# Output gates of a hybrid mLSTM/GLA encoder layer computed with features in partitions and applied after the transpose

## Chip, cores, metric

The kernel runs on one core of one Trainium2 chip. The metric is device time in microseconds (us), the median of several runs. One further execution was taken by the hardware profiler; all rows below come from it.

## What is computed

One layer of a bidirectional encoder over 1024 tokens of width 1024, in float32. The part that matters here is the output of the token mixer:

```python
y_a = sigmoid(a_o) * head_rms_norm(h_fw + h_bw, mlstm_norm)   # 4 heads x 128
y_b = silu(b_r)    * head_rms_norm(o_fw + o_bw, gla_norm)     # 4 heads x 128
y   = concatenate([y_a, y_b], axis=-1)
mix = matmul(y, w_out)
x   = x + rms_norm(mix, norm_mix_post)
```

`a_o` and `b_r` are two 512-column parts of one input projection of the normalised `x`. `head_rms_norm` multiplies each head's 128 features of a token by one number, and by a gain per feature (the kernel folds that gain into `w_out`). A gated MLP with a width-3 convolution follows; the change does not touch it.

## The kernel before

Matmuls in float32 are made of three with a rounded operand each: an operand `v` is split into `vh` (a rounded copy, made by ScalarE, L112) and `vl = v - vh` (VectorE, L113), and the product is `vh*wh + vh*wl + vl*wh`.

**Stages.** First `x` is normalised and transposed to `xh`, `xl` (features in partitions). From then on two generators are interleaved by `_interleave`: `proj()` emits the blocks of the input projection, `mix()` emits the decays, the GLA heads (`gla`), then the mLSTM heads (`mlstm`), and at last the preparation of `w_out` (`out_weights`). Both write to the same five engines, so the projection's matmuls fill TensorE (PE) between the heads' small ones. The tile scheduler then sets the order in which each engine's in-order queue gets its instructions. After that comes the output projection, token tile by token tile (`t` = 0 to 7, 128 tokens each), and then the MLP.

**Blocks of the projection.** `f_block` gives 128 features (in partitions) by 512 tokens: the weights stand still in the array, `x` moves in 512 columns, 8 x 3 = 24 matmuls. `t_block` gives 2 x 128 tokens (in partitions) by 256 features: `x` stands still, the weights move in 256 columns, 2 x 8 x 3 = 48 matmuls. Both fill one PSUM bank. The gates `a_o` and `b_r` are the last 16 blocks of `proj()` and are `t_block`s: `in_gate` takes each bank through tanh on ScalarE (L480) and one more instruction (L482 on ScalarE for the sigmoid, L484 on VectorE for the silu), and after every second block stores 512 KB to `dG` in DRAM, tokens in rows.

**Applying the gates.** `prep(t)` loads the head outputs of one token tile, `yv` (from `dya`, L890, and `dyb`, L891), and its gates `gv` (L893), multiplies by gate and by the head's scale `hr` (eight instructions on VectorE, L897, one for each head), transposes the eight 128x128 blocks on PE in two groups of four (L903) and splits each group from PSUM into `yh`, `yl` for the output matmuls (`oacc`, L1019). In the loop over `t` (L1051 to L1071) the matmuls of tile `t` stand in two halves of 24; `prep(t+1)`'s two groups of transposes are put after the first half and in the middle of the second; after tile `t`, `post(t)` computes the norm (gain L984, power on GpSimd L1032, residual L1040, a second power) and `gates(t+2)` starts the loads of tile `t+2`. `scaled` writes `om` (L989, needs the second power); `finish` transposes it (L997).

**Buffers.** `yv` and `om` share one tag with two buffers. From tile 2 on they alternate, so all of `yv(2)`, `yv(3)`, ... lie in the same buffer, and the load of `yv(t+1)` has to wait for the last reader of `yv(t)`. `gv` has one buffer. All loads and stores around here are issued by SyncE's queue (SP), in order.

```python
yv = ow["p"].tile([P, D], F32, name="yv", tag="yv", bufs=2)
gv = ow["p"].tile([P, D], F32, name="gv", tag="gv", bufs=1)
m = owp.tile([P, D], F32, name="om", tag="yv", bufs=2)
```

Of the kernel before, what the change touches and what calls it, by code (L numbers as in the profile page):

```python
# [13 lines left out]
ALU = mybir.AluOpType  # L14
# [42 lines left out]
def tile_encoder_layer(  # L57
# [24 lines left out]
    dG = [scratch(f"dG{i}", [512, D]) for i in range(2)]  # L82
# [28 lines left out]
    def split(hi, lo, src):  # L111
        nc.scalar.copy(out=hi, in_=src)  # L112
        nc.vector.tensor_tensor(out=lo, in0=src, in1=hi.bitcast(F32), op=ALU.subtract)  # L113
# [294 lines left out]
    def ahead(b=1):  # L408
        c = next(groups, None) if b == 1 else None
        if c is not None:  # L410
            ready.append(wprep(w_in, ((c, 256),)))
# [58 lines left out]
    def in_gate(c0, off, silu):  # L470
        for g in range(2):
            wh, wl = ready.pop(0)
            yield
            for q in range(4):
                if q % 2 == 0:
                    s = stg.tile([P, 4, 256], F32, name="stg")
                acc = yield from t_block(wh, wl, q)
                ahead(q)
                v = s[:, 2 * (q % 2):2 * (q % 2) + 2, :]
                nc.scalar.activation(v, acc, AF.Tanh, scale=0.5)  # L480
                if not silu:
                    nc.scalar.activation(v, v, AF.Identity, bias=one)  # L482
                else:
                    nc.vector.scalar_tensor_tensor(out=v, in0=v, scalar=1.0, in1=acc, op0=ALU.add, op1=ALU.mult)  # L484
                if q % 2:
                    nc.sync.dma_start(dG[q // 2].rearrange("(t p) n -> p t n", p=P)[:, :, off + 256 * g:off + 256 * g + 256], s)
                    if silu and g == 1:
                        done["half"] = True
                yield
# [398 lines left out]
    def prep(t):  # L888
# [3 lines left out]
        gv = ow["p"].tile([P, D], F32, name="gv", tag="gv", bufs=1)  # L892
        nc.sync.dma_start(gv, dG[t // 4][(t % 4) * P:(t % 4 + 1) * P, :])  # L893
        for i in range(2):
            for h in range(H):
                hs = slice(512 * i + P * h, 512 * i + P * h + P)
                nc.vector.scalar_tensor_tensor(out=yv[:, hs], in0=gv[:, hs], scalar=hr[:, t, i, h:h + 1], in1=yv[:, hs], op0=ALU.mult, op1=ALU.mult)  # L897
        ys[t] = []
        for g in range(2):
# [8 lines left out]
            split(yh, yl, pt)  # L908
            ys[t].append((yh, yl))

    def proj():
# [9 lines left out]
        yield from in_gate(C_BR, 512, True)  # L921
# [410 lines left out]
```

## Time and profile before

| | us |
|---|---|
| median of 3 runs | 1188.94 (1188.13 to 1193.38) |
| the profiled execution | 1186.0 |
| its span, first to last instruction | 1184.2 |
| PE busy | 1149.1 (97%) |
| VectorE (DVE) busy | 880.3 (74%) |
| ScalarE (ACT) busy | 591.4 (50%) |
| GpSimd (POOL) busy | 165.5 (14%) |

The stages by time: normalisation and first projection 0 to 47 us, projection with decays and GLA to about 297, mLSTM to about 412, output weights to about 434, output projection to about 549, MLP to the end. The gates' 16 blocks lie between 270 and 433 us.

In a row of the timeline the columns are start, duration, engine, line, operation, written tile `<-` read tiles, and in brackets how long the engine had been idle and what ended that. PE durations overlap, since matmuls are pipelined: the pace is read from start to start, or from a row that merges a run of matmuls.

### The profile page before, as it was taken

The page shows a single profiled execution, that of the slowest core. Times are in us where ns is not written, and L with a number is a line of the kernel's source. Part 1 is how long each engine was busy: PE and PEld are TensorE (multiplying, and loading weights), DVE is VectorE, ACT ScalarE, POOL GpSimd, SP SyncE. Part 2 cuts the span into 40 slices and gives each one's busy share as a digit, 9 for nine tenths or more (in the row PEclk, how much of TensorE's full clock was granted, in tenths as well). Part 3 has the DMA queues.
Part 4 walks back from the last instruction along what each step waited for, and adds up shares of the span by engine and source line. Part 5 has one row for each costly group of instructions (what it writes and reads, how often), then busy time and mean ns, then how long its engine had stood idle before and what let it go on. Part 6 is the DMA issues. An engine that isn't in the chain of part 4 may idle for free.

```text
span 1184.2 us, 21224 instructions
## 1 busy us (share of the span) xinstructions
PE 1149.1 (97%) x7896; PEld 977.0 (82%) x7896; DVE 880.3 (74%) x1604; ACT 591.4 (50%) x1271; POOL 165.5 (14%) x240
## 2 busy tenths in 40 slices
PE   8999999999999989999999999999999999999997
PEld 7989778888989978777788888888888878888885
DVE  6576679777424567567998888888888877987666
ACT  6572696777556534456444243333434245445451
POOL 1200434665154200010000000000000000000001
PEclk9999999999989989999999999999999999999999
DMA  7453675554787485431144332242323248754345
GB/s 211 140 138 98 172 230 150 149 170 129 195 197 222 153 265 185 159 140 64 36 142 143 125 125 74 96 134 99 105 65 133 98 137 295 252 176 132 80 135 190
DMA packets 134651, 175.77 MB, mean 148 GB/s; under 512 B 24964, under 2 KB 89860, under 8 KB 134548
## 3 DMA queue, kind: packets, MB, share of 16 engines
q1 hardware_dynamic: 134116, 172.58, 47.7%
q0 software_dynamic: 432, 1.84, 0.4%
q8 instruction: 62, 1.02, 0.4%
q14 instruction: 41, 0.34, 0.1%
HBM read 126.78 MB, written 47.53 MB: 147 GB/s over the span
## 4 chain that ended last, share of the span: by engine, by line
PE 76%; DVE 6%; ACT 6%; DMA 5%; issue 3%; POOL 2%; SPq 1%; DVEq 0%; POOLq 0%; ACTq 0%
PE pr L1080 35%; PE pr L1238 17%; PE tacc L182 6%; PE facc L171 6%; PE oacc L1019 4%; PE vacc L262 2%; DMA yv<-dya 1%; DMA oraw<-in_w_out_dram 1%; DMA qq<-dmqq 1%; DVE slots L539 1%; PE sc L658 1%; ACT RB L792 1%; DMA wraw<-in_w_in_dram 1%; POOL RB L788 1%; ACT sq L545 1%
## 5 line engine op out<-in xcount | busy, mean ns | idle before, releaser
L1080 PE MATMUL pr<-T,ah 128*128 128x512 f32 x704 | 217.1, 389 | 1.3 <-DVE G L1118 1.3
L1080 PE MATMUL pr<-B,ah 128*128 128x512 f32 x528 | 162.8, 389 | 0.0
L1080 PEld LDWEIGHTS pr<-T,ah 128*128 128x128 f32 x704 | 132.1, 188 | 29.5 <-DVE G L1118 1.8
L1080 PE MATMUL pr<-T,al 128*128 128x512 f32 x352 | 136.9, 389 | 0.0
L182 PE MATMUL tacc<-wh,xh 128*128 128x256 f32 x448 | 130.6, 292 | 0.0
L182 PE MATMUL tacc<-wl,xh 128*128 128x256 f32 x448 | 130.0, 290 | 0.0
L182 PE MATMUL tacc<-wh,xl 128*128 128x256 f32 x448 | 127.0, 284 | 0.0
L1238 PE MATMUL pr<-dwl,dah 128*128 128x512 f32 x308 | 120.0, 390 | 0.7 <-DVE dwl L113 0.7
L1238 PE MATMUL pr<-dwh,dal 128*128 128x512 f32 x308 | 120.1, 390 | 0.0
L1238 PE MATMUL pr<-dwh,dah 128*128 128x512 f32 x308 | 119.2, 390 | 0.4 <-ACT dah L112 0.4
L1080 PEld LDWEIGHTS pr<-B,ah 128*128 128x128 f32 x528 | 99.0, 188 | 20.5
L1080 PE MATMUL pr<-B,al 128*128 128x512 f32 x264 | 102.7, 389 | 0.0
L112 ACT CAST dah<-ar 128x512 fp32r<-128x512 f32 x77 | 47.8, 622 | 97.2 <-PE pr L1238 44.5
L182 PEld LDWEIGHTS tacc<-wh,xh 128*128 128x128 f32 x448 | 85.5, 191 | 2.7 <-issue 0.2
L182 PEld LDWEIGHTS tacc<-wl,xh 128*128 128x128 f32 x448 | 85.6, 191 | 1.4
L182 PEld LDWEIGHTS tacc<-wh,xl 128*128 128x128 f32 x448 | 85.6, 191 | 0.3
L112 ACT CAST ah<-fraw 128x512 fp32r<-128x512 f32 x64 | 39.6, 619 | 82.0 <-PE pr L1080 53.7
L113 DVE TENSOR_TENSOR dal<-ar,dah 128x512 fp32r<-128x512 f32 x77 | 52.9, 689 | 35.5 <-ACT dah L112 35.4
L1080 PEld LDWEIGHTS pr<-T,al 128*128 128x128 f32 x352 | 66.1, 188 | 13.6
L112 ACT CAST ah<-sa 128x512 fp32r<-128x512 f32 x44 | 27.3, 621 | 84.0 <-DVE sa L960 53.3
L1238 PEld LDWEIGHTS pr<-dwl,dah 128*128 128x128 f32 x308 | 57.8, 188 | 13.1 <-DVE dwl L113 1.1
L1238 PEld LDWEIGHTS pr<-dwh,dah 128*128 128x128 f32 x308 | 57.8, 188 | 12.7 <-ACT dah L112 0.8
(292 smaller groups left out, 2528.8 us busy)
## 6 DMA issues: line engine op xcount, KB each, us to landing
ar<-dA SPq DMA_DIRECT2D x77, 256.0 KB
wraw<-in_w_in_dram SPq DMA_DIRECT2D x48, 256.0 KB
fraw<-in_ffn_w_gate_dram SPq DMA_DIRECT2D x22, 512.0 KB
fraw<-in_ffn_w_up_dram SPq DMA_DIRECT2D x22, 512.0 KB
dA<-s SPq DMA_DIRECT2D x20, 512.0 KB
dA<-sx SPq DMA_DIRECT2D x10, 768.0 KB
Y<-in_ffn_w_down_dram SPq DMA_DIRECT2D x22, 256.0 KB
S<-dS SPq DMA_DIRECT2D x16, 258.0 KB
```

Of the source, the lines that this page charges most:

```text
L112: nc.scalar.copy(out=hi, in_=src)
L113: nc.vector.tensor_tensor(out=lo, in0=src, in1=hi.bitcast(F32), op=ALU.subtract)
L171: nc.tensor.matmul(acc, w[:, k, cs], v[:, k, hs], start=(k == 0 and n == 0), stop=(k == NK - 1 and n == 2))
L182: nc.tensor.matmul(acc[:, i, :], v[:, k, ts], w[:, k, :], start=(k == 0 and n == 0), stop=(k == NK - 1 and n == 2))
L262: nc.tensor.matmul(acc, v[:, k, ts], w[:, k, :], start=(k == 0 and n == 0), stop=(k == NK - 1 and n == 2))
L539: nc.vector.scalar_tensor_tensor(out=sl[rs, o, h, :], in0=sl[rs, c, h, :], scalar=sc(c, h)[rs], in1=sl[rs, o, h, :], op0=ALU.mult, op1=ALU ...
L545: nc.scalar.activation(sq, o[:, h, :], AF.Square, accum_out=ss[:, h:h + 1])
L658: nc.tensor.matmul(sc[bs, h, :], K[:, h, bs], Q[:, h, bs], start=True, stop=True)
L788: nc.gpsimd.tensor_tensor(out=RB, in0=RB, in1=cap.rearrange("p (i o t) -> p i o t", i=2, o=1).broadcast_to([P, 2, H, P]), op=ALU.add)
L1019: nc.tensor.matmul(accs[hf], v[:, j, :], w[:, k, hf * 512:(hf + 1) * 512], start=(k == 0 and n == 0), stop=(k == NK - 1 and n == 2))
L1080: nc.tensor.matmul(acc, A[i][:, k, :], B[b][j][:, k, :], start=(k == 0 and n == 0), stop=(k == 3 and n == 2))
L1238: nc.tensor.matmul(accs[i], o[v][:, ts], o[w], start=(p == 0 and n == 0), stop=(p == NP - 1 and n == 2))
```

## The change

The 16 gate blocks become `f_block`s: 24 matmuls of 512 columns in place of 48 of 256, in the order `hf` (half of the tokens) outside, `j` (128 features) inside. ScalarE's and VectorE's work on each bank is the same in shape and number. `dG` now holds features in rows, 512 tokens in each. In `prep`, `gv` is loaded as 8 blocks of 128 features by 128 tokens, from runs of 512 bytes; the eight VectorE instructions are replaced by one GpSimd instruction of 128x1024 that applies the head scales alone, and by two VectorE instructions (one for each group, 128x512) that multiply the transposed rows in PSUM by the gates and write them into `yv`, in place of what was transposed from there. The split reads them from `yv` in SBUF and no longer from PSUM. So the last reader of `yv` is no longer the transpose but the split.

```diff
-    dG = [scratch(f"dG{i}", [512, D]) for i in range(2)]
+    dG = [scratch(f"dG{i}", [2 * H, P, 512]) for i in range(2)]
...
             wh, wl = ready.pop(0)
             yield
-            for q in range(4):
-                if q % 2 == 0:
-                    s = stg.tile([P, 4, 256], F32, name="stg")
-                acc = yield from t_block(wh, wl, q)
-                ahead(q)
-                v = s[:, 2 * (q % 2):2 * (q % 2) + 2, :]
-                nc.scalar.activation(v, acc, AF.Tanh, scale=0.5)
...
-                if q % 2:
-                    nc.sync.dma_start(dG[q // 2].rearrange("(t p) n -> p t n", p=P)[:, :, off + 256 * g:off + 256 * g + 256], s)
...
+            for hf in range(2):
+                s = stg.tile([P, 2, 512], F32, name="stg")
+                for j in range(2):
+                    acc = yield from f_block(wh, wl, j, hf)
+                    ahead(2 * hf + j)
+                    v = s[:, j, :]
+                    nc.scalar.activation(v, acc, AF.Tanh, scale=0.5)
...
+                    if j:
+                        nc.sync.dma_start(dG[hf][off + 2 * g:off + 2 * g + 2].rearrange("b p t -> p b t"), s)
...
-        gv = ow["p"].tile([P, D], F32, name="gv", tag="gv", bufs=1)
-        nc.sync.dma_start(gv, dG[t // 4][(t % 4) * P:(t % 4 + 1) * P, :])
-        for i in range(2):
-            for h in range(H):
-                hs = slice(512 * i + P * h, 512 * i + P * h + P)
-                nc.vector.scalar_tensor_tensor(out=yv[:, hs], in0=gv[:, hs], scalar=hr[:, t, i, h:h + 1], in1=yv[:, hs], op0=ALU.mult, op1=ALU.mult)
+        gv = ow["p"].tile([P, 2 * H, P], F32, name="gv", tag="gv", bufs=1)
+        nc.sync.dma_start(gv, dG[t // 4][:, :, (t % 4) * P:(t % 4 + 1) * P].rearrange("b p t -> p b t"))
+        yb = yv.rearrange("p (h e) -> p h e", h=2 * H)
+        nc.gpsimd.tensor_tensor(out=yb, in0=yb, in1=hr[:, t].rearrange("p i (h o) -> p (i h) o", o=1).broadcast_to([P, 2 * H, P]), op=ALU.mult)
...
-            split(yh, yl, pt)
+            ym = yv[:, 4 * g * P:(4 * g + 4) * P].rearrange("p (j t) -> p j t", j=4)
+            nc.vector.tensor_tensor(out=ym, in0=pt, in1=gv[:, 4 * g:4 * g + 4, :], op=ALU.mult)
+            split(yh, yl, ym)
...
-        yield from in_gate(C_BR, 512, True)
+        yield from in_gate(C_BR, H, True)
```

In the changed kernel the GpSimd instruction is L895, the transposes are L901 and the gate multiplications L907; lines from L910 on are the same.

The order in which the engines' queues get their instructions moves with it. On PE, at the end of the GLA heads (`sc` are scores, `o` their output), the gate's matmuls stand between the same neighbours, one piece of the difference:

```order
 L658 MATMUL sc<-Q,kz_1446 32x32 x16
 L656 MATMUL sc<-qq,kk 32x32 x16
-L182 MATMUL tacc<-wh,xh 128x256
+L171 MATMUL facc<-xh,wh 128x512
 L701 MATMUL o<-v,Pt 128x128
 L702 MATMUL o<-slots,qd 128x128
```

What moved is the block's form alone: as many steps of a block stand between the heads' matmuls, each with half as many instructions twice as wide.

On SP's queue in the output projection, between the stores of tile 2 and tile 3 (`dx_2`, `dx_3`), with the engines whose semaphores each entry waits for, before:

```order
L1041 DMA dx_2_104<-xr 128x1024 [waits DVE_49]
L893 DMA gv<-dG_68 128x1024 [waits DMAHW6_49,DVE_49]
L1053 DMA xr<-in_x_dram 128x1024 [waits DMAHW3_49,DVE_49,Activation_49]
L890 DMA yv<-dya_82 128x512 [waits DMAHW2_49,DMAHW1_49,PE_49]
L891 DMA yv<-dyb_74 128x512 [waits DMAHW7_49]
L1041 DMA dx_3_105<-xr 128x1024 [waits DMAHW0_49,DVE_49]
```

and now:

```order
L1041 DMA dx_2_104<-xr 128x1024 [waits DMAHW3_49,DVE_49]
L1053 DMA xr<-in_x_dram 128x1024 [waits DMAHW3_49,DVE_49,Activation_49]
L893 DMA gv<-dG_68 128x8x128 [waits DMAHW0_49,DVE_49]
L890 DMA yv<-dya_82 128x512 [waits DMAHW1_49,DMAHW2_49,DVE_49,Pool_49]
L891 DMA yv<-dyb_74 128x512 [waits DMAHW7_49]
L1041 DMA dx_3_105<-xr 128x1024 [waits DVE_49]
```

The load of `gv` moved behind that of `xr`, and the load of `yv` (tile 5) waits for VectorE where it waited for PE.

On GpSimd's queue in the same place there were only the powers (two for each tile, `or`); now the head scales (L895) stand among them:

```order
L1032 TENSOR_TENSOR or<-os_6195,mhalf 128x1
L895 TENSOR_TENSOR yv<-yv,hr 128x1024
L1032 TENSOR_TENSOR or<-os_6208,mhalf 128x1
L1032 TENSOR_TENSOR or<-os_6369,mhalf 128x1
L895 TENSOR_TENSOR yv<-yv,hr 128x1024
L1032 TENSOR_TENSOR or<-os_6382,mhalf 128x1
```

From tile 4 on the head scales of tile `t+2` stand between the first power of tile `t` and its second, for which `om` waits; those of tile 3 stand behind both powers of tile 1.

On VectorE's queue a tile reads as follows before (from `om` of tile 4, `yv_7058` being that of tile 7, `yl` the split of tile 6):

```order
L989 TENSOR_SCALAR om_7000<-xr_6833,or_6926 128x512 x2
L113 TENSOR_TENSOR yl_6997<-pt_6991,yh_6996 128x512
L897 SCALAR_TENSOR_TENSOR yv_7058<-gv_7061,hr_127,yv_7058 128x128 x2
L113 TENSOR_TENSOR yl_7021<-pt_7015,yh_7020 128x512
L984 TENSOR_TENSOR oacc_6965<-oacc_6965,gpost_6026 128x512
L984 TENSOR_TENSOR oacc1_6966<-oacc1_6966,gpost_6026 128x512
L1029 TENSOR_SCALAR os3_7038<-os2_7037 128x1
```

and now (from `om` of tile 2, `yv_6215` being that of tile 4, `B21` part of the MLP's operand):

```order
L989 TENSOR_SCALAR om_6330<-xr_6118,or_6213 128x512 x2
L113 TENSOR_TENSOR B21_1_5872<-n21_5879,B21_0_5871 128x4x128
L907 TENSOR_TENSOR yv_6215<-pt_6320,gv_6218 128x512
L113 TENSOR_TENSOR yl_6326<-yv_6215,yh_6325 128x512
L907 TENSOR_TENSOR yv_6215<-pt_6345,gv_6218 128x512
L113 TENSOR_TENSOR yl_6351<-yv_6215,yh_6350 128x512
L984 TENSOR_TENSOR oacc_6294<-oacc_6294,gpost_5714 128x512
```

The eight products that stood scattered through a tile's work are gone; the two gate multiplications stand directly ahead of the two splits, behind `om`.

## Rows read from the trace of the kernel before

**Rows 1.** Page: the chain that ended last, shares by engine.
```profile
PE 76%; DVE 6%; ACT 6%; DMA 5%; issue 3%; POOL 2%; SPq 1%; DVEq 0%; POOLq 0%; ACTq 0%
```
**Rows 2.** Windows: stretch, length, busy PE, PEld, DVE, ACT, POOL, clock, DMA, GB/s.
```profile
340.00:398.00 58.00, 55.97 (x478) 52.70 (x478) 23.74 (x93) 34.50 (x126) 23.52 (x15) 1.00 0.76 211
...
430.00:436.00 6.00, 1.72 (x8) 1.11 (x7) 4.42 (x10) 2.27 (x4) 0.00 (x0) 0.69 0.96 291
436.00:455.00 19.00, 19.00 (x84) 15.40 (x83) 10.65 (x28) 6.46 (x15) 0.60 (x1) 0.92 0.68 224
...
468.00:522.00 54.00, 51.81 (x256) 42.28 (x255) 32.85 (x87) 26.33 (x79) 4.80 (x7) 1.00 0.49 166
```
**Rows 3.** The tile of 256-wide blocks: operation, count, duration ns min/median/max, first and last start.
```profile
L182 PE MATMUL tacc<-wh,xh x448: 277/283/554, 93.3 to 429.7; 128*128 128x256 f32 x150
...
L480 ACT ACTIVATE stg<-tacc x16: 573/590/598, 274.8 to 432.7; 128x512 f32<-128x512 f32 x16
```
**Rows 4.** Chain of waits, 47 to 125 us: start, duration, runs of blocks.
```profile
62.24 5.47 PE facc L171 x24
...
93.48 14.39 PE tacc L182 x120
```
**Rows 5.** Chain of waits: mLSTM, and one row of the output projection.
```profile
295.61 6.82 PE tacc L182 x57
...
316.19 7.79 DMA RB<-drr
...
346.14 5.44 DMA qq<-dmqq
...
401.06 4.51 PE tacc L182 x36
...
496.26 0.44 PE pt L903 x4
```
**Rows 6.** Timeline of VectorE and PE at the start of the output projection.
```profile
432.86 1.28 DVE L109 SCALAR_TENSOR_TENSOR wol<-oraw,hg,woh 128x1024 fp32r<-128x1024 f32 x1 [1.14 <-ACT woh L108]
434.06 2.18 DVE L897 SCALAR_TENSOR_TENSOR yv<-gv,hr,yv 128x128 f32<-128x128 f32 x8
...
434.51 2.00 PE L903 MATMUL pt<-ident,yv 128*128 128x128 f32 x7 [4.28 <-issue]
436.40 0.79 PE L1019 MATMUL oacc<-woh,yh 128*128 128x512 f32 x1
```
**Rows 7.** Timeline of the output projection: transposes, loads, VectorE.
```profile
467.93 0.49 PE L903 MATMUL pt<-ident,yv 128*128 128x128 f32 x3
...
483.29 0.65 PE L903 MATMUL pt<-ident,yv 128*128 128x128 f32 x2 [1.27 <-DVE os L1029]
...
502.33 0.36 SPq L890 DMA_DIRECT2D yv<-dya  x1
...
506.68 0.61 DVE L897 SCALAR_TENSOR_TENSOR yv<-gv,hr,yv 128x128 f32<-128x128 f32 x2 [4.28 <-DMA yv<-dya]
...
522.27 0.38 PE L903 MATMUL pt<-ident,yv 128*128 128x128 f32 x2
```
**Rows 8.** Groups by line on GpSimd: shapes, count | busy us, mean ns | idle before.
```profile
L788 POOL TENSOR_TENSOR RB<-RB,cin 128x1024 f32<-128x1024 f32 x8 | 20.4, 2550 | 33.8 <-DMA RB<-drr 30.5 <-PE nd L813 3.2
L567 POOL TENSOR_TENSOR D<-S 64x512 f32<-64x512 f32 x16 | 16.8, 1050 | 29.3 <-DMA S<-dS 19.6 <-ACT E L626 5.9 <-ACT th L465 2.5
...
L1032 POOL TENSOR_TENSOR or<-os,mhalf 128x1 f32<-128x1 f32 x16 | 10.9, 679 | 123.9 <-DVE os L1030 123.9
```
**Rows 9.** Timeline of single steps: split on ScalarE, `om`, split on VectorE.
```profile
469.96 0.57 ACT L112 CAST yh<-pt 128x512 fp32r<-128x512 f32 x1
...
471.38 0.88 DVE L989 TENSOR_SCALAR om<-xr,or 128x512 f32<-128x512 f32 x2
...
472.18 0.69 DVE L113 TENSOR_TENSOR yl<-pt,yh 128x512 fp32r<-128x512 f32 x1
```
**Rows 10.** The tile `oacc`: the product with an operand in PSUM.
```profile
L984 DVE TENSOR_TENSOR oacc<-oacc,gpost x16: 683/690/700, 450.8 to 543.2; 128x512 f32<-128x512 f32 x16
```

More of the change, by code (lines that the diff above doesn't have):

```diff
@@ L473, in in_gate @@
             yield
-            for q in range(4):
-                if q % 2 == 0:
-                    s = stg.tile([P, 4, 256], F32, name="stg")
-                acc = yield from t_block(wh, wl, q)
-                ahead(q)
-                v = s[:, 2 * (q % 2):2 * (q % 2) + 2, :]
-                nc.scalar.activation(v, acc, AF.Tanh, scale=0.5)
[L481 to L484, printed above, removed]
-                if q % 2:
-                    nc.sync.dma_start(dG[q // 2].rearrange("(t p) n -> p t n", p=P)[:, :, off + 256 * g:off + 256 * g + 256], s)
-                    if silu and g == 1:
-                        done["half"] = True
-                yield
+            for hf in range(2):
[5 more added lines that the diff above has]
+                    nc.scalar.activation(v, acc, AF.Tanh, scale=0.5)
+                    if not silu:
+                        nc.scalar.activation(v, v, AF.Identity, bias=one)
+                    else:
+                        nc.vector.scalar_tensor_tensor(out=v, in0=v, scalar=1.0, in1=acc, op0=ALU.add, op1=ALU.mult)
+                    if j:
+                        nc.sync.dma_start(dG[hf][off + 2 * g:off + 2 * g + 2].rearrange("b p t -> p b t"), s)
+                        if silu and g == 1:
+                            done["half"] = True
+                    yield
     def chain(*gs):
```

## Prediction
> **What bounds the kernel now.** I read the page first: of the chain that ended last, 76% is PE [rows 1]. But the change lies between 270 and 549 us, so the stretches there count and not the average. Two views show them. The windows give PE 55.97 of 58 us busy between 340 and 398 us at full clock, and 51.81 of 54 between 468 and 522 [rows 2]; so in both stretches there is little idle time on PE. The chain of waits shows what ends last. Before 316 us it runs through runs of gate matmuls (one of 57, 6.82 us). Then it leaves PE: the loads of the mLSTM heads (7.79 and 5.44 us the longest) with GpSimd, ScalarE and VectorE behind them carry it to about 398 us. From 401 to 413 us it is back on gate matmuls [rows 5]. From 413 to 434 us it hangs on the loads and splits of `w_out`, whose last split starts at 432.86 [rows 6]. In the output projection a tile takes 13.6 us on the average: the first transposes of a tile start at 467.93 and, four tiles later, at 522.27 [rows 7]. Pure PE work of a tile is less: 48 matmuls at the pace of 24 in 5.47 us [rows 4] are 10.9 us, and the 16 transposes that belong to it by count, 8 of `yv` and 8 of `om`, at four in 0.44 us [rows 5], make 12.7. The difference is waiting: PE sat 1.27 us until VectorE had the product of one tile ready, and VectorE sat 4.28 us until `yv` had landed, 4.35 us after SP issued it [rows 7]. This is a loop: the load of `yv` needs the buffer that the transposes of the tile before release, the product needs the load, the transposes need the product.
>
> **Part 1, the gate blocks on PE.** Of the 1344 matmuls of 256 columns (three groups of 448) those of 16 banks are gates, 48 to a bank [rows 3]: 768. 120 of them follow each other in 14.39 us, 0.120 each; 24 of 512 columns take 5.47, 0.228 each [rows 4]. So 768 x 0.120 = 92.1 us become 384 x 0.228 = 87.6: 4.5 us of PE time are saved, no more, since two narrow matmuls cost almost what a wide one does. How much of it comes off the end? The gates lie between 270 and 432 us, 162 us; in 82 of them (316 to 398) and in 21 (413 to 434) the chain does not touch PE, which leaves 59 of 162, or 36%: 1.6 us. Elsewhere PE would finish sooner and wait for the same loads. Ends: 0 and -4.5. I take -1.6. ScalarE's and VectorE's instructions on the banks are the same in number and size. The stores of `dG` have runs of 2 KB in place of 1 KB, with the same bytes; I cost that at nothing, hidden by loads that end later.
>
> **Part 2, the start of the output projection.** Now PE idles 4.28 us, VectorE ends the last split of `wol` at 434.14, makes eight products in 2.18 us, and the first output matmul starts at 436.40 [rows 6], 2.26 us behind the split. After the change the head scales are on GpSimd, which is idle there, and PE can transpose early. VectorE instead has the last silu product and the first gate product ahead of it, 0.68 and 0.69 us, as products with a PSUM operand take [rows 10], then ScalarE copies in 0.57 [rows 9]: about 2.0 us with handovers. That is a gain of 0.2. Against it stands the clock: behind the idle time the granted clock was 0.69 of full in 430 to 436 us and 0.92 in 436 to 455 [rows 2], so some 3 us of the matmuls ran at 1.2 GHz. PE now waits about as long, but in two pieces; its return to 2.4 GHz may come later. Between -0.5 and +1.7 (another such stretch), I take +0.5.
>
> **Part 3, the loop of the output projection.** The last reader of `yv` is now the second split, so the next load is issued later; in front of the transposes stands one GpSimd instruction for all eight heads; and GpSimd's queue has that instruction ahead of the second power, for which `om` waits, and `om` stands ahead of the gate products on VectorE. From the end of the head scales of one tile, by rows: power 0.68 [rows 8], two `om` 0.88 [rows 9], one split of the MLP's operand 0.69, gate product 0.69 [rows 10], copy 0.57, split 0.69 [rows 9], gate product 0.69, copy 0.57, split 0.69: 6.15, and with about 0.07 us at each of nine handovers 6.8. Then SP issues both halves and they land: 4.35 for the first [rows 7], some 0.3 more because GpSimd needs the second half too. Then the head scales: the nearest row is the 128x1024 sum on GpSimd, 2.55 us on the mean; the one with a broadcast along its last axis, 64x512 in 1.05, would make 2.1 for twice the length [rows 8]. With 2.4 the loop is 6.8 + 4.65 + 2.4 = 13.9 us, 0.3 more than 13.6. Four rounds: +1.2. Tile 3 is worse, since its head scales stand behind both powers of tile 1: from the transposes of tile 2 there are 6.2 us to the end of tile 1's matmuls (24 and 4 transposes twice), some 6.5 until its second power is done, then 2.4: 15.3, +1.7. Sum +2.9, rounded +3. VectorE loses eight products for two wider ones, about 2.2 us against 1.4, and no longer stands in line behind the load; that relief is in the loop above already, which has no wait of that kind.
> Ends: if `yv` lands in 3.4 us or sooner, PE's 12.7 us bind, -0.9 a tile over five: -4.5. If it takes 6 us and GpSimd 3.8, the loop is 16.7: +15.
>
> The Trainium skill (GPSIMD Engine Reference, section 4.1, Engine selection) speaks against this part: it says that a product of two tensors belongs on VectorE, GpSimd being about twice as slow. The trace has 2.55 us on GpSimd for 1024 columns against 2.18 on VectorE for the eight pieces of 128 [rows 6, 8], a ratio of 1.2 and not 2. By the page the head scales would take 4.4 us and the loop 15.9: +2.3 a tile.
>
> **Sum.** 1184.2 - 1.6 + 0.5 + 3 = 1186.1 of span. The profiled run took 1.8 more than its span, and the median lies 2.9 above that run: 1190.8, say 1191.
>
> **Rivals.** (a) Slower: the loop through the one `yv` buffer becomes the bound. Its place is the wait of SP's load for the second split. It costs the difference between the loop and 13.6 us for five tiles, and it decides from about 15 us on: with 2.2 us a tile, 11 us, and 1199; with the far end, 1203. For it: PE has waited here already, and the load of `yv` and the products are serial. Against it: VectorE is freed, and `xr` is loaded well ahead. Chance 0.27. The page's factor of two for GpSimd ends in this rival, at 1200, and has 0.05 of that chance; the trace speaks against its size, not against its sign.
> (b) Faster: the whole 4.5 us of PE time come off because the mLSTM stretch follows PE after all (it is 97% busy there), and the output projection runs at PE's 12.7 us a tile, 4.5 more: 1180. For it: VectorE's wait on the load, 4.28 us in a tile, goes. Against it: the loads around 316 to 398 us are not touched. Chance 0.15.
> (c) The clock: if PE's waits in each tile grow from 1.3 us towards the 4.28 that stood ahead of the slow stretch, the output projection runs partly at 1.2 GHz; with 3 us lost in each of five tiles, 1206. Nothing of that kind shows between 468 and 522 us, where the clock was 1.00 with waits up to 1.27 [rows 2, 7]. Chance 0.04. The Trainium skill (TensorE: Matmul & The Clock Gate, HAM oscillation — how this bites in real kernels) describes loops that wait on a load in each round and start each round at the lower rate; by it the place to look is here, and this run bears it out for the one wait at 430 us alone.
> (d) The change does nothing measurable on either side, 1189: it lies within the forecast.
>
> **How the numbers follow.** A measurement of this kernel can tell about 0.5%, 6 us: faster is below 1183, slower above 1194.9. The forecast and (d) hold 0.54, nearly all of it within that. Slower is (a) and (c), 0.31; faster is (b), 0.15. The range leaves out the far half of (b), (c) and the end of (a): 1183 to 1202.
>
> **What would show it.** Part 1: 384 matmuls at 0.228 us for the gates, and chain and loads of the mLSTM heads ending within 2 us of where they ended. Part 2: the first output matmul 2 us behind the last split of `wol`. Part 3: GpSimd's 128x1024 product between 2.1 and 2.6 us; the load of `yv` issued behind the second split; a tile about 14 us, the first of them 15. I am wrong if a tile takes under 13 us (the buffer was no bound), over 15 (rival a), or if the mLSTM stretch moves by more than 3 us, by a new order of its queues.

## The result, and the profile after

The changed kernel took 1195.88 us in the median of 22 runs, the kernel before 1189.12 in 22 runs beside it: a ratio of 1.0050, 95% interval 1.0035 to 1.0065. A second comparison on another chip (the first experiment) gave 1.0021, interval 0.9994 to 1.0049. So the first comparison puts the cost at 4 to 8 us, the second at -1 to 6; the forecast was 2 us, with slower as the likelier sign and 1202 as the far end.

The page of the changed kernel has the same bound as [rows 1]: a longer span, and almost the same shares of the chain that ended last.

```profile
span 1192.6 us, 20459 instructions
PE 75%; DVE 7%; ACT 6%; DMA 5%; issue 3%; POOL 3%; SPq 1%; DVEq 0%; POOLq 0%; ACTq 0%
```

Windows of the changed kernel (columns as in [rows 2]). Between 340 and 415 us, where the clock was full before, the mean granted clocks are now 0.94 and 0.80, and between 398 and 415 us PE is busy for 11.68 of 17 us, where it was for 16.83. The output projection's middle (468 to 522) looks like the row of before: 50.77 against 51.81 us of PE.

```profile
340.00:398.00 58.00, 55.30 (x335) 45.45 (x334) 24.18 (x93) 31.07 (x112) 19.93 (x13) 0.94 0.64 179
398.00:415.00 17.00, 11.68 (x64) 9.96 (x65) 6.54 (x25) 8.00 (x33) 4.59 (x3) 0.80 0.47 127
...
468.00:522.00 54.00, 50.77 (x251) 41.36 (x250) 38.62 (x67) 27.60 (x80) 12.45 (x12) 1.00 0.51 167
```

The window of the kernel before that [rows 2] does not have:

```profile
398.00:415.00 17.00, 16.83 (x151) 16.00 (x150) 9.48 (x38) 9.81 (x36) 3.03 (x3) 1.00 0.22 82
```

Four marks cut a profile into stages: the last head scale of the mLSTM heads (the end of the last L548 on GpSimd), the last gate matmul, the first output matmul and the last one. In this pair of profiles the whole loss lies ahead of the output projection:

| us of the span | before | changed |
|---|---|---|
| last head scale ready | 413.7 | 424.0 |
| last gate matmul ends | 430.2 | 439.3 |
| first output matmul | 436.4 | 445.4 |
| last output matmul ends | 541.9 | 550.4 |
| output projection, the last two's difference | 105.5 | 105.0 |
| from there to the end of the span | 642.3 | 642.2 |

That reads like a refutation of the prediction's third part. It is one pair of profiles, and the experiments show how far such a pair can be trusted.

**Time lost to the clock.** Each run comes with its span and the mean granted clock over it. (1 - clock) x time is a measure of what the run lost by PE at 1.2 GHz in place of 2.4: an upper one, since time in which PE had nothing to do counts too. Over the 22 runs of the changed kernel it explains most of the scatter: the run of 1201.19 us had a clock of 0.981, the run of 1187.63 one of 0.992; the correlation of the measure with the time is 0.85, the slope 0.83 us a us. I use it beside every comparison below.

| kernel (runs) | mean us | (1 - clock) x time | the rest |
|---|---|---|---|
| before, beside a_again, e1, e2, e5 (34) | 1189.8 | 12.0 | 1177.8 |
| changed, first comparison (22) | 1195.5 | 17.0 | 1178.5 |
| a_again: changed (12) | 1193.0 | 14.3 | 1178.7 |
| e1_blocks (12) | 1188.8 | 13.4 | 1175.5 |
| e2_apply (12) | 1192.8 | 14.1 | 1178.7 |
| e5_narrow (12) | 1193.4 | 14.0 | 1179.4 |
| before, beside e6, f1, f2 (29) | 1189.9 | 11.5 | 1178.4 |
| e6_gvout (12) | 1189.5 | 15.4 | 1174.2 |
| f1_fill (12) | 1190.6 | 10.9 | 1179.7 |
| f2_gvfill (12) | 1188.3 | 14.0 | 1174.3 |
| before, beside g1, g2, g3 (24) | 1190.1 | 11.0 | 1179.1 |
| g1_gvstore (7) | 1182.8 | 12.3 | 1170.5 |
| g2_bstore (12) | 1188.0 | 10.8 | 1177.2 |
| g3_gvstorefill (12) | 1183.7 | 12.0 | 1171.7 |
| before, beside g4 (11) | 1190.0 | 12.3 | 1177.7 |
| g4_gatelate (6) | 1180.6 | 11.2 | 1169.4 |

The standard error of "the rest" is 0.3 to 0.9 us, that of the clock column 0.5 to 1.5. The changed kernel's rest is that of the kernel before, within 1 us. What it lost stands for the most part in the clock column: 2.3 of 3.2 us in a_again, and some 5 of 6 in the first comparison, set against the 34 runs of before.

### The profile page after: what moved, and what is told of

The parts are those of the page before. It is cut to its first block, busy times and chain, and to the rows that moved or that the text cites. A ratio compares the mean times of both kernels' runs of the same rounds, so it can differ in the third digit from the quotient of the medians.

```text
span 1192.6 us, 20459 instructions
## 1 busy us (share of the span) xinstructions
PE 1149.9 (96%) x7512; PEld 958.4 (80%) x7512; DVE 883.2 (74%) x1556; ACT 592.0 (50%) x1271; POOL 181.6 (15%) x248
## 4 chain that ended last, share of the span: by engine, by line
PE 75%; DVE 7%; ACT 6%; DMA 5%; issue 3%; POOL 3%; SPq 1%; DVEq 0%; POOLq 0%; ACTq 0%
PE pr L1080 34%; PE pr L1238 16%; PE facc L171 8%; PE oacc L1019 6%; PE tacc L182 4%; PE vacc L262 2%; DMA yv<-dyb 1%; PE nd L809 1%; PE nd L813 1%; DVE slots L539 1%; POOL yv L895 1%; DMA S<-dS 1%; POOL RB L788 1%; DMA wraw<-in_w_in_dram 1%; DVE T L113 1%
## 5 line engine op out<-in xcount | busy, mean ns | idle before, releaser
L171 PE MATMUL facc<-xh,wh 128*128 128x512 f32 x256 | 104.3, 407 | 0.0
L171 PE MATMUL facc<-xh,wl 128*128 128x512 f32 x256 | 103.4, 404 | 0.0
L171 PE MATMUL facc<-xl,wh 128*128 128x512 f32 x256 | 103.3, 403 | 0.0
L1238 PEld LDWEIGHTS pr<-dwh,dah 128*128 128x128 f32 x308 | 57.8, 188 | 12.7 <-ACT dah L112 0.7
L1238 PEld LDWEIGHTS pr<-dwh,dal 128*128 128x128 f32 x308 | 57.8, 188 | 12.6 <-DVE dal L113 0.8
L1080 PEld LDWEIGHTS pr<-B,al 128*128 128x128 f32 x264 | 49.6, 188 | 10.3
```

The costliest lines, as they stand in the source:

```text
L171: nc.tensor.matmul(acc, w[:, k, cs], v[:, k, hs], start=(k == 0 and n == 0), stop=(k == NK - 1 and n == 2))
L1080: nc.tensor.matmul(acc, A[i][:, k, :], B[b][j][:, k, :], start=(k == 0 and n == 0), stop=(k == 3 and n == 2))
L1238: nc.tensor.matmul(accs[i], o[v][:, ts], o[w], start=(p == 0 and n == 0), stop=(p == NP - 1 and n == 2))
```

## Experiments

The trace pointed to the mLSTM stretch, the prediction to the output projection. So the theories are: **L**, the loop through the `yv` buffer, as predicted; **O**, the new blocks change the order of the queues in the mLSTM stretch, and that is the loss; **V**, that stretch varies from run to run in any kernel. **K** (the cost is clock) and **S** (what stands ahead of the last head's loads in SP's queue) came out of the first results.

**The two kernels again.** Both unaltered, for a second profile of each.

> The changed kernel unaltered, for a second profile and for times beside the others. All theories: ratio to the kernel before 1.004 to 1.007 (about 1195 us). Theory O (order): the last head scale of the mLSTM heads is ready at about 423 us of the span (413 before), 10 us late, and the output projection from its first matmul to the last of its tiles takes no longer than before (105 us). Theory L (loop through the yv buffer): the output projection takes 5 to 8 us longer than before, the mLSTM heads no longer.

> The kernel before, unaltered, for a second profile of it. Theory V (the mLSTM stretch varies from run to run, whatever the kernel): the last head scale of the mLSTM heads is ready somewhere between 414 and 422 us of the span, with a PE wait of 2 us or more near 395 us, as in the kernel with old blocks and new application, whose queues there have the order of before. Theory O (order): it ends at 413 to 415 us again, without such a wait, and only kernels with another order end later.

Measured: a_again 1.0021 (0.9994 to 1.0049), below the 1.004 that all theories had; one run of before 1188.38 us. In a_again the last head scale is ready at 417.8 us, in b_again at 416.0 (before: 413.7). So the mLSTM stretch of one and the same kernel ends up to 6 us earlier or later from run to run. Theory V holds as far as that (b_again's wait below, 1.95 us, is just under the 2 that it had), and the 10 us of the first pair were mostly such a difference. PE's wait for the scores (`sr`) of the last head is the row to compare; first before (timeline of PE):

```profile
392.51 1.13 PE L799 MATMUL sr<-qq,kko 64*128 64x128 f32 x8 [0.51 <-issue]
```

the same in b_again:

```profile
394.81 1.13 PE L799 MATMUL sr<-qq,kko 64*128 64x128 f32 x8 [1.95 <-issue]
```

in a_again:

```profile
396.35 2.05 PE L799 MATMUL sr<-qq,kko 64*128 64x128 f32 x8 [6.13 <-issue]
```

and in the first profile of the changed kernel:

```profile
403.32 2.04 PE L799 MATMUL sr<-qq,kko 64*128 64x128 f32 x8 [5.61 <-issue]
```

The wait is short in the kernel before and long in the changed one, both times; and where it is long, the same eight matmuls take 2.04 us in place of 1.13, that is, they run at 1.2 GHz. The output projection took 108.1 us in a_again and 105.1 in b_again: there theory L's sign shows, with 3 us where it had 5 to 8.

**The change cut in two.** e1_blocks has the new gate blocks and the old application, e2_apply the old blocks and the new application. In both the gates are read in an order that is not theirs, so the values of the output are not the reference's.

```diff
# e1_blocks, against the changed kernel: prep() as before, but for the load
-        nc.sync.dma_start(gv, dG[t // 4][(t % 4) * P:(t % 4 + 1) * P, :])
+        nc.sync.dma_start(gv, dG[t // 4].rearrange("b p n -> (b p n)").rearrange("(r c) -> r c", c=D)[(t % 4) * P:(t % 4 + 1) * P, :])
# e2_apply, against the kernel before: prep() as after, but for the load
-        nc.sync.dma_start(gv, dG[t // 4][:, :, (t % 4) * P:(t % 4 + 1) * P].rearrange("b p t -> p b t"))
+        nc.sync.dma_start(gv, dG[t // 4].rearrange("a (b n) -> (a b) n", n=512).rearrange("(b p) n -> b p n", p=P)[:, :, (t % 4) * P:(t % 4 + 1) * P].rearrange("b p t -> p b t"))
```

> New gate blocks (512 columns, features in partitions) with the old application (eight products on VectorE, gates not transposed). The gates are read in an order that is not theirs, so the values of the output are not the reference's; instructions, bytes and waits are those of a working kernel. Theory O: the loss stays, ratio 1.004 to 1.009, the last head scale of the mLSTM heads again 8 to 11 us later than before. Theory L: the loss is gone, and the 4.5 us that PE saves show in part, ratio 0.996 to 0.999.

> Old gate blocks (256 columns, tokens in partitions) with the new application (head scales on GpSimd, gates multiplied behind the transposes). The gates are read in an order that is not theirs, so the values of the output are not the reference's; instructions, bytes and waits are those of a working kernel. Theory O: no loss, ratio 0.998 to 1.002, the mLSTM heads end where they did before. Theory L: the loss is all here, ratio 1.004 to 1.008, tiles of 14 us and more.

Measured: e1 0.9985 (0.9957 to 1.0013), e2 1.0012 (0.9988 to 1.0036). By the ratios alone the cut does not decide: e1 lies in theory L's range, but e2 in theory O's, below the 1.004 that theory L had. In means against the 34 runs of before on that chip, e1 is 0.9 us faster (95%: 2.2 us either way) and e2 3.0 us slower (1.5 either way); the two differ by 3.9 (2.2 either way). So theory O, that the loss comes with the blocks, is not borne out: e1 shows no cost. Its rest is 2.3 us below that of before, as less work on PE would make it; 1.4 us more in its clock column are within the scatter. By the means the cost lies with the application, as the prediction had it, though the intervals of the two ratios overlap.

e1's last head scale is at 418.0 us, with the changed kernel's order in SP's queue; e2's is at 420.9, in a queue that has before's order up to the output projection: once more the scatter of that stretch. e2's profiled run is its slowest (1197.02 us), so its stages weigh less than the others'.

**Narrow matmuls, new layout.** The gate blocks are built of 48 matmuls of 256 columns, features in partitions.

```diff
+        for i in range(2):
+            hs = slice(hf * 512 + i * 256, hf * 512 + i * 256 + 256)
...
+                    nc.tensor.matmul(acc[:, i * 256:(i + 1) * 256], w[:, k, cs], v[:, k, hs], start=(k == 0 and n == 0), stop=(k == NK - 1 and n == 2))
```

> The changed kernel with its gate blocks made of 48 matmuls of 256 columns in place of 24 of 512; layout and application are the new ones. With this the queues of the mLSTM stretch have the same order as before the change. Theory O: the loss goes although PE has 4.5 us more to do, ratio 0.998 to 1.002, last head scale of the mLSTM heads within 3 us of before. A theory that the new layout of the gates (stores of 2 KB runs, loads of 512 bytes) or the application costs the time: ratio stays at 1.005 to 1.010.

Measured: 1.0028 (1.0006 to 1.0051), between the two ranges that were set. With before's order in the mLSTM stretch and before's number of matmuls the loss is still there. Theory O is out; the width of the matmuls and the order that comes with it are not what makes the changed kernel slower.

**Releasing `yv` earlier.** The gate product is written over `gv` and not over `yv`. Then `yv`'s last readers are the transposes again, as before the change, and only the load of `gv`, which has a whole tile of time, waits for the second split.

```diff
-            ym = yv[:, 4 * g * P:(4 * g + 4) * P].rearrange("p (j t) -> p j t", j=4)
+            ym = gv[:, 4 * g:4 * g + 4, :]
```

> The changed kernel with the products of gates and transposed rows written over the gates (gv) and not over yv, so that yv's last readers are the transposes again, as before the change. Theory L (loop through yv): PE's wait for the head scales of tile 3, 1.8 to 3.4 us in the four profiles with the new application, falls under 1 us, the output projection takes 102.5 to 105 us in place of 105 to 110, ratio to before 0.998 to 1.002. If the application's cost lies elsewhere (start of the output projection, work on VectorE): the output projection stays at 105 or more, ratio 1.002 to 1.005.

Measured: 0.9999 (0.9976 to 1.0021); the output projection takes 100.8 us, against 105.0, 108.1, 109.7, 107.1 and 104.2 in the five profiles with the product in `yv` (changed, a_again, e2, e5, f1). So what holds up the output projection is what e6 takes away. (The kernels built on e6 take 98.6 to 101.2 us there, and in all five every tile from tile 3 on takes 12.7 to 12.8.) The chain of waits of a_again has the loop in full ahead of tile 3: copy, second split, SP, load, GpSimd, transposes.

```profile
464.99 0.64 ACT yh L112
...
465.64 0.70 DVE yl L113
...
466.40 0.34 SPq L890
...
466.79 5.53 DMA yv<-dyb
...
472.48 2.46 POOL yv L895
...
474.98 1.12 PE pt L901 x4
```

The transposes of tile 3 waited 3.23 us there (timeline of PE in a_again),

```profile
474.98 1.12 PE L901 MATMUL pt<-ident,yv 128*128 128x128 f32 x4 [3.23 <-POOL yv L895]
```

and 1.81 us in the first profile of the changed kernel:

```profile
478.75 0.66 PE L901 MATMUL pt<-ident,yv 128*128 128x128 f32 x4 [1.81 <-POOL yv L895]
```

In e6 (timeline of PE) they follow without a wait, and the next tile's 12.8 us later (487.88 less 475.12), against the 12.7 that the prediction counted as PE's own work:

```profile
475.12 0.60 PE L901 MATMUL pt<-ident,yv 128*128 128x128 f32 x4
...
487.88 0.60 PE L901 MATMUL pt<-ident,yv 128*128 128x128 f32 x4
```

The edit moved a second thing with it. In the changed kernel the head scales of tile 3 stand on GpSimd behind both powers of tile 1, and in its first profile they started, at 476.80, right behind the second power (timeline of GpSimd):

```profile
476.29 0.55 POOL L1032 TENSOR_TENSOR or<-os,mhalf 128x1 f32<-128x1 f32 x1 [2.54 <-DVE os L1030]
```

In e6 the scheduler put them ahead of both powers; they start at 470.87, and the first of the two powers follows:

```profile
472.93 0.55 POOL L1032 TENSOR_TENSOR or<-os,mhalf 128x1 f32<-128x1 f32 x1 [0.16 <-DVE os L1030]
```

In a_again, e2 and e5 the load came last for tile 3, but GpSimd stood for it only 0.45 to 0.82 us behind the second power. In f1, where the second power stands behind the head scales, GpSimd stood 3.1 us ahead of them and they started 5.3 us behind the issue of the load, as they did in the changed kernel (5.2), and tile 3 took 14.8 us all the same. So theory L is shown: the late load holds up tile 3 by itself. The place behind both powers would have held it nearly as long, and what e6 gains by each of the two was not separated.

e6's rest is 4.2 us below before's. But its clock column is 3.9 above, so that the time is only even. What it gained in work, the clock took.

**Filling PE's wait ahead of the output projection.** 16 matmuls of 512 columns, with results that nothing uses, in the bank that the first transposes write. f1 is the changed kernel with them, f2 is e6, g3 is g1 (below).

```diff
+            if t == 0 and g == 0:
+                with tc.issue_after(lastmm[0].ins):
+                    for n in range(NFILL):
+                        nc.tensor.matmul(pt.rearrange("p j t -> p (j t)"), ow["h"][:, 0, 0:P], ow["h"][:, 0, 512:1024], start=True, stop=True)
```

> The changed kernel with 16 matmuls of 512 columns more, behind the last gate block, whose results nothing uses; they stand in the bank that the first transposes write and fill most of the 4.7 to 5.5 us in which PE waits there. Theory K (the time that the change costs is mostly granted clock): the stretch at 1.2 GHz at the start of the output projection (1.7 to 3.4 us lost in the profiles so far) goes, ratio to before 0.999 to 1.003 against 1.002 to 1.005 without. If the clock there costs nothing or falls for another reason: the clock falls again or the time stays, ratio 1.002 to 1.006.

> Both: products written over gv, and the 16 unused matmuls behind the last gate block. If theories L and K hold and add up: ratio to before 0.995 to 0.999, output projection under 104 us with no clock loss at its start. If one of them fails: as the other alone.

> As with products over gv and late stores, and 16 unused matmuls of 512 columns behind the last gate block, which fill most of PE's wait ahead of the output projection. Theory K (clock): 1.5 to 3.4 us less than without the unused matmuls, ratio 0.990 to 0.996, no clock loss at the start of the output projection. If the matmuls only delay the transposes: the same as without, or up to 2 us more.

Measured: f1 1.0007 (0.9980 to 1.0034), f2 0.9993 (0.9965 to 1.0021) against 0.9999 for e6, g3 0.9942 (0.9918 to 0.9966) against 0.9936 for g1. The clock does what theory K says: in none of the three profiles does it fall where the output projection starts, while it had in all the others. First windows of the changed kernel:

```profile
440.00:445.00 5.00, 0.21 (x2) 0.00 (x0) 3.74 (x5) 2.75 (x4) 1.85 (x1) 1.00 1.03 293
445.00:449.00 4.00, 3.90 (x12) 3.14 (x13) 1.79 (x3) 0.62 (x1) 0.04 (x1) 0.57 0.94 228
```

window of e6:

```profile
440.00:448.00 8.00, 4.81 (x15) 3.95 (x16) 4.16 (x6) 1.17 (x2) 3.79 (x2) 0.57 0.73 228
```

and of f1, whose first output matmul starts at 440.7:

```profile
440.00:448.00 8.00, 8.00 (x40) 6.76 (x40) 5.49 (x9) 2.34 (x4) 0.05 (x1) 1.00 0.99 336
```

The time does not clearly follow. f1 lies in the range that theory K had, but its interval holds a_again's 1.0021 as well; f2 stays above the 0.995 to 0.999 that was set, and neither f2 nor g3 gains against the kernel without the matmuls. In f1 the first output matmul came 4.8 us behind the last split of `wol` (435.9 to 440.7), where it came 3.0 behind in the changed kernel: the scheduler now put all transposes of tile 1 ahead of it, and they wait for tile 1's head scales. One wait was exchanged for another. In these three profiles the fall there goes with PE's wait; that filling it pays, the runs do not show.

**What holds up the last head's loads.** In kernels with the wide blocks PE waits 4.4 to 6.6 us for the scores of the last head (changed, a_again, e1, e6, f1, f2, g1, g3), in those with narrow ones 0.5 to 3.8 (before, b_again, e2, e5, g2). Here the clock of the two kernels parts: around the end of this wait it fell to 1.2 GHz, for 7 to 10 us in those eight profiles and for 7 in e2 and e5 (waits of 3.82 and 2.52 us), but not in before, b_again and g2 (0.51 to 1.95). At half the clock that is 3 to 5 us in the clock column. Why e2 and e5 wait longer than the kernel before, with its order in SP's queue, was not found. SP's timeline in the changed kernel shows what stands ahead of that head's loads (`kko`, `RB`, `RI`, `qq`): behind the loads of gate weights (`wraw`) its queue stood from 384.3 to 390.35 us, until the store of a finished head's output (`dya`) could go.

```profile
380.96 3.30 SPq L150 DMA_DIRECT2D wraw<-in_w_in_dram  x3
390.35 0.34 SPq L549 DMA_DIRECT2D dya<-hs  x1
391.44 0.37 SPq L486 DMA_DIRECT2D dG<-stg  x1
391.86 0.47 SPq L780 DMA_DIRECT2D kko<-dmk  x1
...
393.76 0.42 SPq L784 DMA_DIRECT2D RB<-drr  x1
...
395.90 1.23 SPq L525 DMA_DIRECT2D qq<-dmqq  x2
```

In the kernel before, the key load and the first `RB` load stand ahead of that store:

```profile
379.70 0.48 SPq L780 DMA_DIRECT2D kko<-dmk  x1
380.29 0.52 SPq L784 DMA_DIRECT2D RB<-drr  x1
...
385.01 0.36 SPq L549 DMA_DIRECT2D dya<-hs  x1
```

No line of the change touches these loads or that store. Their order goes with the shape of the gate blocks next to them: e1 has the changed kernel's, e5 that of before. g1_gvstore is e6 with each `dya` store behind the next head's loads, g2_bstore the kernel before with the same, as a control.

```diff
-            nc.sync.dma_start(dst, o.rearrange("p h e -> p (h e)"))
+            held.append((dst, o))
...
                 if c + 2 < NC:
                     decays(c + 2)
+                    with tc.issue_after(last[0].ins):
+                        flush()
```

> Products written over gv, and besides each store of the mLSTM heads' outputs (dya) put behind the loads of the head three further on, in SP's queue. Theory S (with the wide blocks PE comes to the last heads early and waits 4.4 to 6.4 us near 395 us for loads that stand behind such a store, and the clock falls after that wait): the wait falls under 3 us, the last head scale is ready at 413 to 418 us, and the ratio to before goes from 1.000 to 0.993 to 0.997. If the wait has another cause (the DMA queues themselves, GpSimd, another entry ahead of the loads): it stays at 4 to 6 us and the ratio at 0.998 to 1.002.

> The kernel before with its stores of the mLSTM heads' outputs put behind the loads of the head three further on, as a control. Theory S: little to gain, since PE waits 0.5 to 2 us there and the stores stand behind most of those loads already: ratio 0.997 to 1.001. If late stores alone help any kernel: ratio under 0.996.

Measured: g1 0.9936 (0.9912 to 0.9960), g2 0.9982 (0.9965 to 0.9999). g1's time came as theory S said, but the wait did not: 5.67 us. So where the late stores gain is not shown; in the control they gain 0.2%, within its range. The waits of PE in that profile (total, times, longest) have it,

```profile
PE sr L808 <- DVE rd L831: 5.7, 1, 5.7
```

the waits of SP name the next one in the queue, a store of gates, for which it stood 7.3 us,

```profile
SPq L486 <- DVE rs_v L547: 7.3, 1, 7.3
```

and SP's timeline shows that store ahead of the `RB` loads:

```profile
381.69 0.37 SPq L486 DMA_DIRECT2D dG<-stg  x1
382.16 0.40 SPq L793 DMA_DIRECT2D RB<-drr  x1
```

So g4_gatelate holds the stores of the gates back in the same way:

```diff
-                        nc.sync.dma_start(dG[hf][off + 2 * g:off + 2 * g + 2].rearrange("b p t -> p b t"), s)
+                        heldg.append((dG[hf][off + 2 * g:off + 2 * g + 2].rearrange("b p t -> p b t"), s))
+                        if not hold[0]:
+                            flushg()
```

> As the kernel with products over gv and late stores of the heads' outputs, and now the stores of the gates (dG), while mLSTM heads remain, also behind the next head's loads: one of them stood between the key load and the RB loads of the last head and held SP's queue for 7.3 us. Theory S in its second form (it is what stands ahead of the last head's loads in SP's queue that makes PE wait near 390 us): PE's wait there falls from 5.7 us to under 3 us, ratio to before 0.988 to 0.993. If these loads are late for another reason: the wait stays at 4 to 6.5 us and the ratio at 0.993 to 0.996.

Measured: 0.9918 (0.9893 to 0.9943), 1179.46 us in the median, against 1190.05 for before in the same runs. PE's wait for the last head is down to 1.28 us (timeline of PE):

```profile
398.44 1.13 PE L816 MATMUL sr<-qq,kko 64*128 64x128 f32 x8 [1.28 <-DVE rd L838]
```

In this one profile the wait is down as theory S has it: what holds up these loads is what stands ahead of them in SP's queue. The clock still fell behind the wait, for 3.4 us. In time g4 and g1 can't be told apart, since their intervals overlap, so what the shorter wait is worth is not shown. How much of the long wait comes from the order, and how much from PE being there earlier with wide blocks, was not separated. Both g1 and g4 beat both kernels: by 0.6% and 0.8% against before.

## Why the prediction was right, point by point

**The total.** 1191 was forecast, with 1183 to 1202 around it; 1195.88 and 1192.95 came. The sign was the likelier one of the two, and the place that was named, the application's path to the transposes, is shown by e1, e2 and e6. That the total came out inside the range is in part luck. In work (its rest) the changed kernel lost about 1 us, where the sum has 1.9; most of the loss is clock, for which the sum had only the 0.5 of part 2.

**Part 1 (-1.6 us).** 31 gate matmuls follow each other in 7.06 us in the chain of the changed kernel, 0.228 each, as forecast:

```profile
295.78 7.06 PE facc L171 x31
```

e1 gives -0.9 us for the part, with an interval from -5 to +1.5, and -2.3 without the clock. What failed is the test that I set: "chain and loads of the mLSTM heads ending within 2 us of where they ended". The last head scale came on the average 3.4 us later with wide blocks (420.9 in the changed kernel, a_again, e1, e6, f1 and f2) than with narrow ones (417.5 in before, b_again, e2 and e5). With a standard error of about 2 us that is likely and not shown, and the two profiles of before alone lie 2.3 us apart, so one pair could not decide the test. The gates then end 15.35 us behind it and not 16.5. The step behind it was that the loads of that stretch "are not touched". They are, by the order of SP's queue. The order is shown; the delay from it is only likely. The prediction named "a new order of its queues" as what would make it wrong there and did not look for it.

**Part 2 (+0.5 us).** The first output matmul was to come 2.0 us behind the last split of `wol`; it came 3.0 behind in the changed kernel and 3.4 in a_again, where [rows 6] have 2.26. The missing term is in the chain of the changed kernel: the first transposes of tile 1 stand ahead of that matmul on PE, and wait for a load of 6.44 us and for GpSimd.

```profile
435.76 0.76 SPq L890
...
436.57 6.44 DMA yv<-dyb
...
443.14 1.91 POOL yv L895
...
445.10 0.55 PE pt L901 x3
```

In e2 and e5 that matmul stands ahead of tile 1's transposes, and came 1.35 and 1.76 us behind the split. The clock's return cost no more than before: (1 - clock) x length of the stretch, from windows of 1 us, is 1.7 us behind this wait in the changed kernel and 3.4 in before, b_again and a_again.

**Part 3 (+3 us).** The mechanism held, but what it costs lies in tile 3 alone. Tile 3, forecast at 15.3 us (the terms given add up to 15.1), took 14.7 in the changed kernel (464.1 to 478.75), 16.1 in a_again, 16.5 in e5, where the profiles with the old application have 12.7 to 12.8: 1.9 to 3.7 us more. The later tiles took 12.9 to 14.3 us in these profiles, where I had 13.9; their mean is 13.5 in the five profiles with the product in `yv`, 13.5 in the four with the old application and 12.8 in e6. So the loop bound these tiles as it had before, no longer, and the +1.2 for four rounds did not show. Two of its terms were too large: the load, 4.65 us from the first issue to the second landing, where the timeline and the chain have 3.98 (499.31 to 503.29) and 3.38 (513.00 to 516.38), if 5.92 for tile 3 in a_again; and GpSimd's product, 1.90 us in the median in place of 2.4. One was missing, VectorE's stops beside GpSimd (last section). The tile `yv` of the changed kernel (columns as in [rows 3]):

```profile
L907 DVE TENSOR_TENSOR yv<-pt,gv x16: 677/684/692, 442.9 to 537.1; 128x512 f32<-128x512 f32 x16
...
L113 DVE TENSOR_TENSOR yl<-yv,yh x16: 678/692/1802, 444.3 to 538.8; 128x512 fp32r<-128x512 f32 x16
...
L895 POOL TENSOR_TENSOR yv<-yv,hr x8: 1894/1897/2409, 430.1 to 530.0; 128x1024 f32<-128x1024 f32 x8
```

The far end of the bound for a tile without the loop, 12.7 us of PE alone, is what e6 shows. In the output projection as a whole the new application costs 1.9 us: 106.8 in the mean of its five profiles with the product in `yv`, 104.95 in the four with the old application (before, b_again, e1, g2); +2.9 was forecast. The single values, 104.2 to 109.7 and 103.4 to 105.9, overlap. The factor of two that the Trainium skill (GPSIMD Engine Reference, section 4.1, Engine selection) gives for products of two tensors on GpSimd would have made 4.4 us of the 1.90, so for this product it is not borne out: eight pieces on VectorE took 2.18 [rows 6], and two VectorE products of 128x512 would take 1.37 (an estimate, two of L907), a ratio of 1.4.

**The rivals.** (a) asked for tiles over 15 us; only tile 3 was, in three of the five profiles. (b) needed PE as the bound on both sides and did not come with the change as it stands; with the loop and the stores out of the way (g1, g4) the time of 1180 that it gave does come, but those kernels moved more than its two terms, so that the number does not show its sum. (c), at 0.04, was the one that I mis-sized: not a fall in every tile, but more time at 1.2 GHz behind PE's longer waits, in the mLSTM stretch and behind tile 3's wait, is where most of the measured loss stands. The step that failed is that the sum had no term for it, since the windows of [rows 2] showed the clock at 1.00 in these stretches. The one from 340 us starts right behind a fall in the same profile, while PE did the head matmuls that the prediction's reading of the chain (off PE from 316 to 398 us) left out:

```profile
333.00:340.00 7.00, 7.00 (x38) 6.10 (x38) 2.00 (x8) 3.18 (x10) 3.96 (x3) 0.52 0.89 236
```

(This is a window of the kernel before.) A mean over runs would have shown 11 to 12 us of clock loss in the kernel before, and a scatter of 3 us with it.

## What to carry to other kernels

An instruction that is changed in one stage can move the queues of stages that no line of the diff touches, above all a store that ends up ahead of the next step's loads on an in-order DMA queue: compare the order of every queue around the longest waits, and not only where the change is. Work written over a buffer makes its last reader later; writing it over the operand that is needed latest (`gv` here) shortened the output projection by some 6 us, with GpSimd's order changed beside it, though the time of e6 alone was only even with before's. One profile gave the stages of this kernel to within some 5 us only: use the runs' mean clock to split a small difference into work and clock before explaining it.

## What the runs showed of the hardware that was not expected

**VectorE and GpSimd block each other.** The two halves of `om` take 0.88 us on VectorE [rows 9]; in the changed kernel they once took 2.51, beside GpSimd's head scales. The timeline of VectorE,

```profile
476.87 2.51 DVE L989 TENSOR_SCALAR om<-xr,or 128x512 f32<-128x512 f32 x2 [0.73 <-POOL or L1032]
```

and that of GpSimd:

```profile
476.80 1.89 POOL L895 TENSOR_TENSOR yv<-yv,hr 128x1024 f32<-128x1024 f32 x1
```

An instruction of one column, which the changed kernel's VectorE timeline has at 0.15 us,

```profile
472.90 0.15 DVE L1030 SCALAR_TENSOR_TENSOR os<-os,os 128x1 f32<-128x1 f32 x1
```

took 1.57 us in e6 in the same way (timeline of VectorE,

```profile
471.22 1.57 DVE L1030 SCALAR_TENSOR_TENSOR os<-os,os 128x1 f32<-128x1 f32 x1
```

and of GpSimd):

```profile
470.87 1.90 POOL L895 TENSOR_TENSOR yv<-yv,hr 128x1024 f32<-128x1024 f32 x1 [6.34 <-DMA yv<-dyb]
```

VectorE stood until GpSimd was done. The other way round, GpSimd's product took 2.41 us in place of 1.90 where a split on VectorE had started just ahead of it (516.51 and 516.53 us, changed kernel). The Trainium skill (SBUF — State Buffer, section Who interferes with whom) states it: a VectorE instruction in a two-port mode or with two operands in SBUF and a GpSimd instruction that reads SBUF share a pair of ports, and the later one is blocked whole. The trace agrees; the prediction left this cost of the move to GpSimd out, 1.4 to 1.6 us of VectorE in the two cases shown.

**The clock falls behind PE's waits, but not behind each.** In a_again PE was nearly idle from 390 to 396 us and then ran at 1.2 GHz until 403; behind the 3.23 us ahead of tile 3 it did so until 478 (windows of a_again):

```profile
390.00:396.00 6.00, 0.21 (x1) 0.00 (x0) 2.75 (x9) 2.21 (x9) 0.87 (x1) 0.71 1.02 196
396.00:403.00 7.00, 6.66 (x22) 5.69 (x23) 1.30 (x2) 3.15 (x12) 3.71 (x3) 0.51 0.40 155
...
474.00:478.00 4.00, 3.02 (x10) 2.60 (x11) 1.13 (x2) 0.62 (x1) 0.92 (x1) 0.57 0.41 131
```

In the changed kernel it did not fall behind tile 3's wait of 1.81 us, nor in e5 behind one of 3.35. The stretch at 1.2 GHz behind the first wait for a head differed as well: 7 us in the kernel before, 14 in the changed one, none in b_again, where that wait was 0.84 us. What decides that was not tried.
